# Where the operands of TensorE's products lie in a partition: places modulo 256 bytes instead of modulo 128

## The chip, the cores and the metric

One core of one Trainium2 chip runs the whole kernel. The metric is the device time of one execution in microseconds (us), the median of several runs. The profile is of one further execution.

## The reference

A two-layer decoder trunk on x of 256 x 1024 in float32. Every layer is a mixer between two half-step SwiGLU feed-forward blocks, each with an RMSNorm ahead of it; a last RMSNorm ends it. Layer 0 mixes with a chunked spatial gating unit, layer 1 with stick-breaking attention on keys and values that are made from x ahead of layer 1.

```python
D_MODEL = 1024; SEQ = 256; D_FF = 2816; D_A = 2048; SB_HEADS = 16; SB_KV_HEADS = 4
def swiglu(h, w_in, w_out):
    gate, up = jnp.split(h @ w_in, 2, axis=-1)
    return (jax.nn.silu(gate) * up) @ w_out
for i in range(2):
    if i == 1:
        k, v = split(rms_norm(x, kv_norm) @ w_kv)
    x = x + 0.5 * swiglu(rms_norm(x, ffn_norm[i, 0]), ffn_w_in[i, 0], ffn_w_out[i, 0])
    h = rms_norm(x, mix_norm[i])
    if i == 0:
        u, v = split(gelu(h @ a_w_in)); v = spatial(layer_norm(v))   # W_s causal in chunks of 128
        x = x + (u * v) @ a_w_out
    else:
        x = x + stick_breaking_attention(h @ b_w_q, k, v) @ b_w_o
    x = x + 0.5 * swiglu(rms_norm(x, ffn_norm[i, 1]), ffn_w_in[i, 1], ffn_w_out[i, 1])
return rms_norm(x, final_norm)
```

## The kernel before

x stands transposed in SBUF, as xT of 128 partitions x 8 chunks x 256 tokens. Every float32 operand of a product is split into two parts, hi (rounded to the type float32r) and lo (the rest), and `mm3` (lines 156 to 162) makes one product out of three on TensorE: the lo part of the first operand by the hi part of the second (L160), hi by lo (L161) and hi by hi (L162); the first operand is the loaded one. In each of the three one operand is **loaded** into the array (128 columns of 4 bytes, 512 bytes of each partition) and the other is **moved** through it (256 columns, 1024 bytes of each partition, or 512 columns, 2048 bytes). In this text "a product" is one such instruction pair, a weight load (PEld in the profile) and a matmul (PE).

Worked out from the loops, the kernel has 7540 products with 256 moved columns and 294 with 512, besides 157 small float32 ones (transposes, column sums, the spatial mix).

Weights come in 333 units of 128 x 1024 float32 through the class `Weights`: SP issues the DMA into `raw` seven units ahead, ACT makes `whi` (L85) and VectorE `wlo` (L87) up to five units ahead, and TensorE takes unit after unit in a fixed order. The stages in order are the feed-forward blocks a (tags ga, ua, ya), then the v half of the gating unit (v), its u half with mix and output (uu, mix, ys), block b, the key and value projections (kT and v again), block c, attention with the q and o projections (q, z, at, o, yo) and block d (gd, ud, yo).

Which operand is moved differs by stage. In the first half of a feed-forward block (`project`) the activations xnh and xnl are moved and the weights loaded; in its second half (`Residual.add`) hh and hl are moved and the weights loaded. In the v stage, in the value projection (`project_rows`) and in the second half of block d (`out_add`) it is the weights that are moved, and the activations are loaded.

All tiles are laid out one after another in each partition, by pools in the order of the code. So a tile's place in the partition follows from the sizes of those ahead of it, and two small pools (`gap`), the padded size of `eps` and the argument `place` of `Weights.add` shift it. What counts for the change is the place modulo 256 bytes. Before, it is this (a weight buffer has 4224 bytes, 16.5 times 256, so that neighbouring buffers differ by 128):

| tile | place modulo 256, before | after |
|---|---|---|
| xnh, xnl (moved; loaded in the v stage) | 128 | 192 |
| hh, hl, q, a0, a1 (moved; q and block d's h loaded) | 192 | 192 |
| whi, wlo of the in-weights, loaded | 64 or 192 by buffer | 80 |
| whi, wlo of the out-weights, loaded | 0 or 128 by buffer | 80 |
| whi, wlo, moved: v stage and values | 64 or 192 by buffer | 48 |
| whi, wlo, moved: block d, out | 0 or 128 by buffer | 48 |
| xkh, xkl, oT (moved; xk loaded for the values) | 192 | 192 |
| kz (moved) | 128 | 48 |
| vd (loaded) | 128 | 80 |

The place of the moved operand less that of the loaded one, modulo 256, is thus 64 or 192 before in 7722 products, 0 in 56 and 128 in 56. The 0 and 128 are those of the key and value projections and of the small mask product in attention (later by identr).

Of the kernel before, what the change touches and what calls it, by code (L numbers as in the profile page):

```python
# [8 lines left out]
F32 = mybir.dt.float32  # L9
F32R = mybir.dt.float32r  # L10
# [5 lines left out]
P = 128  # L16
T = 256
D = 1024
KC = D // P
DFF = 2816  # L20
NPAIR = DFF // 256
DA = 2048
UNIT = 1024
# [3 lines left out]
RAW_AHEAD = 7  # L27
SPLIT_AHEAD = 5
WARM = 6, 10

# [6 lines left out]
class Weights:  # L39
# [14 lines left out]
        self.loaded = 0  # L54
        self.split = 0

    def add(self, source, place=0):
        self.sources.append(source)
        self.places.append(place)
        return len(self.sources) - 1  # L60
# [5 lines left out]
    def run_to(self, load, split):  # L66
        nc = self.nc
        while self.loaded < min(load, len(self.sources)):
            i = self.loaded
            raw = self.pools[0].tile([P, UNIT], F32, tag="raw", name=f"raw{i}")  # L70
            src = self.sources[i]
            view = raw if len(src.shape) == 2 else raw.rearrange("p (k c) -> p k c", k=src.shape[1])
            nc.sync.dma_start(view, src)
            self.raw[i] = raw
            self.loaded += 1
        while self.split < min(split, len(self.sources)):
            i = self.split
            raw = self.raw.pop(i)
            hi, lo = (
                pool.tile([P, UNIT + 32], F32R, tag=f"w{p}", name=f"w{p}{i}")[:, self.places[i] : self.places[i] + UNIT]  # L80
                for pool, p in zip(self.pools[1:], ("hi", "lo"))
            )
            for c in range(0, UNIT, self.piece):
                cc = slice(c, c + self.piece)
                ins = nc.scalar.copy(hi[:, cc], raw[:, cc])  # L85
                self.order(ins)
                ins = nc.vector.tensor_sub(lo[:, cc], raw[:, cc], hi[:, cc].bitcast(F32))  # L87
                self.order(ins)
                if self.behind:
                    self.keep_order(ins)  # L90
                    self.behind -= 1
            self.parts[i] = hi, lo
            self.split += 1
# [10 lines left out]
def trunk(  # L104
# [22 lines left out]
    out = out[0]  # L127

    def gap(name, size):


        pool = ctx.enter_context(tc.tile_pool(name=name, bufs=1))
        pool.tile([P, size // 4], F32, name=f"{name}t")

    const = ctx.enter_context(tc.tile_pool(name="const", bufs=1))
    act = ctx.enter_context(tc.tile_pool(name="act", bufs=1))
    gap("gapw", 32)
    rawp = ctx.enter_context(tc.tile_pool(name="rawp", bufs=7))
    hip = ctx.enter_context(tc.tile_pool(name="hip", bufs=9))
    lop = ctx.enter_context(tc.tile_pool(name="lop", bufs=9))  # L140
    gap("gaph", 128)
    hp = ctx.enter_context(tc.tile_pool(name="hp", bufs=4))
    scr = ctx.enter_context(tc.tile_pool(name="scr", bufs=8))
    small = ctx.enter_context(tc.tile_pool(name="small", bufs=3))
# [9 lines left out]
    def scratch(name, width=512):  # L154
        return scr.tile([P, width], F32, tag="scr", name=name, padded_shape=[P, 516])

    def mm3(o, a, b, first, last):

        (ah, al), (bh, bl) = a, b
        nc.tensor.matmul(o, al, bh, start=first, stop=False, skip_group_check=True)  # L160
        nc.tensor.matmul(o, ah, bl, start=False, stop=False, skip_group_check=True)  # L161
        nc.tensor.matmul(o, ah, bh, start=False, stop=last, skip_group_check=True)  # L162
# [15 lines left out]
    W = Weights(tc, rawp, hip, lop)  # L178

    def cols(w, c0, kh):  # L180
        return w[kh * 512 : (kh + 1) * 512, c0 : c0 + 256].rearrange("(k p) c -> p k c", p=P)

    def rows(w, r0):
        return w[r0 : r0 + P, :]

    def plan_in_out(n, ins, w_out):


        steps = {}
        for j in range(n + 1):  # L190
            if j < n:
                steps["in", j] = [[W.add(cols(w, c0 + 256 * j, kh)) for w, c0 in ins] for kh in range(2)]
            if j:
                steps["out", j - 1] = [W.add(rows(w_out, 256 * (j - 1) + P * m), 16) for m in range(2)]
        return steps

    def plan_ffn(i, s):
        return plan_in_out(NPAIR, [(ffn_w_in[i, s], 0), (ffn_w_in[i, s], DFF)], ffn_w_out[i, s])

    plan00 = plan_ffn(0, 0)  # L200
    plan_v = [[W.add(cols(a_w_in[0], DA + 256 * j, kh)) for kh in range(2)] for j in range(8)]
    plan_u = {}
    for step in U_STEPS:
        kind, j = step
        if kind == "in":
            plan_u[step] = [W.add(cols(a_w_in[0], 256 * j, kh)) for kh in range(2)]
        elif kind == "out":
            plan_u[step] = [W.add(rows(a_w_out[0], 256 * j + P * m), 16) for m in range(2)]
    plan01 = plan_ffn(0, 1)
    plan_kv = [[W.add(cols(w_kv, 256 * j, kh)) for kh in range(2)] for j in range(2)]  # L210
    plan10 = plan_ffn(1, 0)
    plan_q = [[W.add(cols(b_w_q[0], 256 * j, kh)) for kh in range(2)] for j in range(4)]
    plan_o = [W.add(rows(b_w_o[0], P * b), 16) for b in range(8)]
    plan11 = plan_ffn(1, 1)


    xin = {}
# [17 lines left out]
    for i, group in enumerate(ROWS):  # L235
        r0 = 0
        for name, ap in group:
            n = ap.shape[0]
# [16 lines left out]
    def warm_up(n):  # L255

        bank = gbank("warm")
        for _ in range(n):
            W.order(nc.tensor.matmul(bank[:, :P], ones, ones, start=True, stop=True))


    def transpose_gains(i):
        n = gT[i].shape[1]
        pgain = gbank(f"pgain{i}")
        nc.tensor.transpose(pgain[:, :n], rowsb[i], ident[:n, :n])
        nc.vector.tensor_copy(gT[i], pgain[:, :n])
# [34 lines left out]
            nc.scalar.activation(s, xT[:, d, :], AF.Square)  # L301
            nc.gpsimd.tensor_add(acc, acc, s)  # L302

    eps = const.tile([P, 1], F32, name="eps", padded_shape=[P, 32])
    nc.vector.memset(eps, RMS_EPS)

    def newton(o, root, v, w):
# [36 lines left out]
    def load_x(hf):  # L344

        for d in range(hf * 4, hf * 4 + 4):
            ptr = ybank(f"ptr{d}")
            for tt in range(2):
                W.order(
                    nc.tensor.transpose(  # L350
                        ptr[:, tt * P : (tt + 1) * P], xin[tt, hf][:, (d % 4) * P : (d % 4 + 1) * P], ident
                    )
                )
            if d % 2:
                W.order(nc.vector.tensor_copy(xT[:, d, :], ptr[:, :T]))
            else:
                W.order(nc.scalar.copy(xT[:, d, :], ptr[:, :T]))
        for d in range(hf * 4, hf * 4 + 4):
            prepare(d, [(("ffn", 0), xnh, xnl)], False)
            if d % 2 == 0:  # L360
                s = scratch(f"sqx{d}", T) if d else acc
                nc.gpsimd.tensor_mul(s, xT[:, d, :], xT[:, d, :])
                if d:
                    nc.gpsimd.tensor_add(acc, acc, s)
            if d == 2:
                W.piece = 512
                W.run_to(0, 1)
                W.piece = UNIT
        W.run_to(0, 2)
        for d in range(hf * 4 + 1, hf * 4 + 4, 2):  # L370
            square(d)

    W.strict = True
    warm_up(WARM[0])
    transpose_gains(0)
    load_x(0)
    warm_up(WARM[1])

# [8 lines left out]
    class Residual:  # L387
# [8 lines left out]
        def add(self, w, h, first, last, ds=range(KC)):  # L396
            for d in ds:
                mm3(
                    self.at(d), tuple(t[:, d * P : (d + 1) * P] for t in w), h, first and d % 2 == 0, last
                )  # L400
# [234 lines left out]
    for kind, j in U_STEPS:  # L635
# [4 lines left out]
        else:  # L640
            h = hs.pop(j)
            for m in range(2):
                w = W.get(plan_u["out", j][m], UNIT)
# [8 lines left out]
    att = ExitStack()  # L652
    at = att.enter_context(tc.tile_pool(name="att", bufs=1))
    at.tile([P, 8], F32, name="gapk")
    kz = [at.tile([P, 4, 2, T], F32R, name=f"kz{p}") for p in "hl"]
    vd = [at.tile([P, 2, 4, 2, 64], F32R, name=f"vd{p}") for p in "hl"]
    at.tile([P, 16], F32, name="gapx")
    xkh = at.tile([P, KC, T], F32R, tag="bigh", name="xkh")
    xkl = at.tile([P, KC, T], F32R, tag="bigl", name="xkl")
    for t in kz:  # L660
        nc.gpsimd.memset(t.bitcast(F32), 0.0)

    laterf = at.tile([P, 2, P], F32, name="laterf")
    later = at.tile([P, 2, P], F32R, name="later")
    identr = at.tile([P, P], F32R, name="identr")
    nc.gpsimd.memset(laterf, 0.0)
# [1 line left out]
        laterf, laterf, pattern=[[0, 2], [-1, P]], compare_op=ALU.is_gt, fill=-(2.0**100), base=0, channel_multiplier=1  # L668
# [201 lines left out]
    for tt in range(2):  # L870
# [20 lines left out]
        r = small.tile([P, 2], F32, tag="fr", name=f"fr{tt}")  # L891
# [40 lines left out]
```

## Time and profile before

| | |
|---|---|
| median of 3 runs | 982.39 us (981.85 to 983.96) |
| the profiled execution | 983.58 us |
| its span, first to last instruction | 981.9 us |
| TensorE (PE) busy | 968.1 us, 99% |
| VectorE (DVE) busy | 641.8 us, 65% |
| ScalarE (ACT) busy | 503.4 us, 51% |
| GpSimd (POOL) busy | 70.4 us, 7% |
| HBM traffic | 181 GB/s over the span |

A matmul's own duration in the profile is modelled and reaches over the start of the next, so it says little. What TensorE spends on a product is read from the starts in the timeline, or from the number of instructions in a window.

### The profile page before, as it was taken

How to read it: one execution, taken by the hardware profiler on the slowest of the kernel's cores; microseconds unless marked ns; L12 is line 12 of the kernel's file. 1: busy time of each engine (PE TensorE's matmuls, PEld its weight loads, DVE VectorE, ACT ScalarE, POOL GpSimd, SP SyncE). 2: the span in 40 equal slices, each digit the busy share in tenths (PEclk: the TensorE clock that was granted, in tenths of full speed). 3: DMA queues.
4: the chain of work that ended last, by engine and by line, in shares of the span. 5: the costliest groups of instructions: out<-in, count | busy, mean ns of one | idle time of the engine just before them, and what ended most of it. 6: DMA issues, size and time to landing. Idle time of an engine off the chain costs nothing.

```text
span 981.9 us, 19299 instructions
## 1 busy us (share of the span) xinstructions
PE 968.1 (99%) x8058; PEld 949.4 (97%) x8058; DVE 641.8 (65%) x823; ACT 503.4 (51%) x691; POOL 70.4 (7%) x98
## 2 busy tenths in 40 slices
PE   8999999999999999999999999999999999999996
PEld 8999999999999999999999999999998999999996
DVE  6865675675866775656569756565689775565653
ACT  6643434474644564444448534343488774444433
POOL 4100000020000310000002000000032120000002
PEclk9999999999999999999999999999999999999999
DMA  9967566647555457575654866666644346656511
GB/s 293 331 196 210 173 194 190 191 136 236 176 190 173 151 175 212 175 211 178 211 176 138 258 190 194 190 193 190 201 150 129 101 148 196 208 179 205 182 43 44
DMA packets 135207, 179.55 MB, mean 183 GB/s; under 512 B 5624, under 2 KB 119376, under 8 KB 135120
## 3 DMA queue, kind: packets, MB, share of 16 engines
q1 hardware_dynamic: 134768, 177.76, 58.1%
q8 instruction: 63, 1.03, 0.4%
q0 software_dynamic: 192, 0.52, 0.2%
q14 instruction: 24, 0.20, 0.1%
q10 hardware_dynamic: 160, 0.05, 0.0%
HBM read 176.73 MB, written 1.05 MB: 181 GB/s over the span
## 4 chain that ended last, share of the span: by engine, by line
PE 90%; DVE 5%; ACT 2%; DMA 1%; issue 1%; SPq 0%; POOL 0%; ACTq 0%; DVEq 0%; POOLq 0%
PE yo L160 3%; PE yo L162 3%; PE yo L161 3%; PE gc L162 2%; PE uc L162 2%; PE gc L161 2%; PE gc L160 2%; PE uc L161 2%; PE gb L162 2%; PE gb L161 2%; PE gb L160 2%; PE uc L160 2%; PE ub L162 2%; PE ub L161 2%; PE ub L160 2%; PE ud L162 2%
## 5 line engine op out<-in xcount | busy, mean ns | idle before, releaser
L85 ACT CAST whi<-raw 128x1024 fp32r<-128x1024 f32 (+1 forms) x333 | 342.3, 1044 | 379.6 <-issue 194.5
L87 DVE TENSOR_TENSOR wlo<-raw,whi 128x1024 fp32r<-128x1024 f32 (+1 forms) x333 | 401.6, 1223 | 195.1 <-ACT whi L85 194.2
L302 POOL TENSOR_TENSOR acc<-acc,sq 128x256 f32<-128x256 f32 x39 | 33.9, 869 | 375.5 <-ACT sq L301 373.6
L161 PE MATMUL ga<-xnl,whi 128*128 128x256 f32 x176 | 49.1, 279 | 1.0 <-DVE xnl L289 1.0
L160 PE MATMUL ga<-xnh,wlo 128*128 128x256 f32 x176 | 49.9, 283 | 0.0
L160 PE MATMUL ua<-xnh,wlo 128*128 128x256 f32 x176 | 48.8, 277 | 0.5 <-DVE wlo L87 0.5
L160 PE MATMUL ya<-hha,wlo 128*128 128x256 f32 x176 | 48.9, 278 | 0.2 <-DVE xT L411 0.2
L160 PE MATMUL yc<-hhc,wlo 128*128 128x256 f32 x176 | 48.9, 278 | 0.1
L160 PE MATMUL gb<-xnh,wlo 128*128 128x256 f32 x176 | 49.0, 278 | 0.0
L160 PE MATMUL gd<-xnh,wlo 128*128 128x256 f32 x176 | 48.9, 278 | 0.0
L160 PE MATMUL yb<-hhb,wlo 128*128 128x256 f32 x176 | 48.9, 278 | 0.0
L160 PE MATMUL gc<-xnh,wlo 128*128 128x256 f32 x176 | 48.9, 278 | 0.0
L162 PE MATMUL ga<-xnh,whi 128*128 128x256 f32 x176 | 48.9, 278 | 0.0
L162 PE MATMUL gc<-xnh,whi 128*128 128x256 f32 x176 | 48.8, 277 | 0.0
L162 PE MATMUL uc<-xnh,whi 128*128 128x256 f32 x176 | 48.8, 277 | 0.0
L161 PE MATMUL gc<-xnl,whi 128*128 128x256 f32 x176 | 48.7, 277 | 0.0
L162 PE MATMUL gd<-xnh,whi 128*128 128x256 f32 x176 | 48.7, 277 | 0.0
L162 PE MATMUL gb<-xnh,whi 128*128 128x256 f32 x176 | 48.7, 277 | 0.0
L162 PE MATMUL ud<-xnh,whi 128*128 128x256 f32 x176 | 48.7, 277 | 0.0
L161 PE MATMUL gb<-xnl,whi 128*128 128x256 f32 x176 | 48.7, 277 | 0.0
L161 PE MATMUL uc<-xnl,whi 128*128 128x256 f32 x176 | 48.7, 277 | 0.0
L161 PE MATMUL gd<-xnl,whi 128*128 128x256 f32 x176 | 48.7, 277 | 0.0
(294 smaller groups left out, 3327.2 us busy)
## 6 DMA issues: line engine op xcount, KB each, us to landing
raw<-in_ffn_w_in_dram SPq DMA_DIRECT2D x176, 512.0 KB, 4.6
raw<-in_ffn_w_out_dram SPq DMA_DIRECT2D x88, 512.0 KB, 4.2
raw<-in_a_w_in_dram SPq DMA_DIRECT2D x32, 512.0 KB, 4.4
raw<-in_a_w_out_dram SPq DMA_DIRECT2D x16, 512.0 KB, 3.3
raw<-in_b_w_q_dram SPq DMA_DIRECT2D x8, 512.0 KB, 4.5
raw<-in_b_w_o_dram SPq DMA_DIRECT2D x8, 512.0 KB, 4.2
raw<-in_w_kv_dram SPq DMA_DIRECT2D x4, 512.0 KB, 4.5
xin<-in_x_dram SPq DMA_DIRECT2D x4, 256.0 KB, 4.9
```

The lines of the kernel that those rows point to most:

```text
L85: ins = nc.scalar.copy(hi[:, cc], raw[:, cc])
L87: ins = nc.vector.tensor_sub(lo[:, cc], raw[:, cc], hi[:, cc].bitcast(F32))
L160: nc.tensor.matmul(o, al, bh, start=first, stop=False, skip_group_check=True)
L161: nc.tensor.matmul(o, ah, bl, start=False, stop=False, skip_group_check=True)
L162: nc.tensor.matmul(o, ah, bh, start=False, stop=last, skip_group_check=True)
L302: nc.gpsimd.tensor_add(acc, acc, s)
```

## The change

Every weight buffer becomes 4352 bytes, 17 times 256, so that all weight buffers have the same place modulo 256, and a unit is put 208 bytes into its buffer if it will be loaded (LOADED) or 176 bytes if it will be moved (MOVED). The padding of eps and the pool gaph move the activations to 192. The tiles kz and vd for the keys and values become one tile each, with 176 and 208 bytes ahead of their content. In all 7818 products but the 16 of the mask, the moved operand's place less the loaded one's is then 112 modulo 256. Since kz, vd and the buffers need more room, the tile laterf (the mask before rounding) is no longer a tile of its own: it takes one of the eight scratch buffers.

```diff
+LOADED, MOVED = 52, 44
...
-    def add(self, source, place=0):
+    def add(self, source, place=LOADED):
...
-                pool.tile([P, UNIT + 32], F32R, tag=f"w{p}", name=f"w{p}{i}")[:, self.places[i] : self.places[i] + UNIT]
+                pool.tile([P, UNIT + 64], F32R, tag=f"w{p}", name=f"w{p}{i}")[:, self.places[i] : self.places[i] + UNIT]
...
-    gap("gaph", 128)
+    gap("gaph", 64)
...
-                steps["out", j - 1] = [W.add(rows(w_out, 256 * (j - 1) + P * m), 16) for m in range(2)]
+                steps["out", j - 1] = [W.add(rows(w_out, 256 * (j - 1) + P * m), place) for m in range(2)]
...
-    plan_v = [[W.add(cols(a_w_in[0], DA + 256 * j, kh)) for kh in range(2)] for j in range(8)]
+    plan_v = [[W.add(cols(a_w_in[0], DA + 256 * j, kh), MOVED) for kh in range(2)] for j in range(8)]
...
-            plan_u[step] = [W.add(rows(a_w_out[0], 256 * j + P * m), 16) for m in range(2)]
+            plan_u[step] = [W.add(rows(a_w_out[0], 256 * j + P * m)) for m in range(2)]
...
+        [W.add(cols(w_kv, 256 * j, kh), place) for kh in range(2)] for j, place in enumerate((LOADED, MOVED))
...
-    plan_o = [W.add(rows(b_w_o[0], P * b), 16) for b in range(8)]
-    plan11 = plan_ffn(1, 1)
+    plan_o = [W.add(rows(b_w_o[0], P * b)) for b in range(8)]
+    plan11 = plan_ffn(1, 1, MOVED)
...
-    eps = const.tile([P, 1], F32, name="eps", padded_shape=[P, 32])
+    eps = const.tile([P, 1], F32, name="eps", padded_shape=[P, 48])
...
-    kz = [at.tile([P, 4, 2, T], F32R, name=f"kz{p}") for p in "hl"]
-    vd = [at.tile([P, 2, 4, 2, 64], F32R, name=f"vd{p}") for p in "hl"]
+    kzs = at.tile([P, 2 * 8 * T + 64], F32R, name="kz")[:, 44 : 44 + 2 * 8 * T]
+    vds = at.tile([P, 2 * 16 * 64 + 64], F32R, name="vd")[:, 52 : 52 + 2 * 16 * 64]
...
-    laterf = at.tile([P, 2, P], F32, name="laterf")
+    laterf = scratch("laterf", T).rearrange("p (n s) -> p n s", n=2)
```

On TensorE, VectorE, ScalarE and SP the instructions stand in the same order as before, with the same shapes. Only POOL's order moves, in one place: at the end of the gating unit, where POOL prepares the attention's mask (laterf, later) and adds up the squares of the new x (acc) for block b's norm. Before, with what each waits for:

```order
L661 MEMSET kzh 128x2048 [waits DVE_49,DMAHW4_49,PE_49,Activation_49]
L661 MEMSET kzl 128x2048
L666 MEMSET laterf 128x256
L671 CAST identr<-ident 128x128
L667 AFFINE_SELECT laterf<-laterf 128x256 [waits Pool_49]
L670 CAST later<-laterf 128x256 [waits Pool_49]
L302 TENSOR_TENSOR acc<-acc,sq_4100 128x256 [waits Activation_49]
L302 TENSOR_TENSOR acc<-acc,sq_4112 128x256 [waits Activation_49,Pool_49]
```

And now the same place in the changed kernel, from the fifth of the seven sums on:

```order
L307 TENSOR_TENSOR acc<-acc,sq_4148 128x256 [waits Activation_49,Pool_49]
L307 TENSOR_TENSOR acc<-acc,sq_4160 128x256 [waits Activation_49,Pool_49]
L674 MEMSET laterf 128x256 [waits DVE_49]
L675 AFFINE_SELECT laterf<-laterf 128x256 [waits Pool_49]
L307 TENSOR_TENSOR acc<-acc,sq_4172 128x256 [waits Activation_49]
L678 CAST later<-laterf 128x256 [waits Pool_49]
```

The two instructions that fill laterf have moved from ahead of the seven sums to between the sixth and the last, and the first of them now waits for VectorE, which used that scratch buffer before. The cast to later follows the last sum.

## Rows read from the trace of the kernel before

**Rows 1.** The page: busy times, slices of the clock, costliest groups.
```profile
PE 968.1 (99%) x8058; PEld 949.4 (97%) x8058; DVE 641.8 (65%) x823; ACT 503.4 (51%) x691; POOL 70.4 (7%) x98
...
PE 90%; DVE 5%; ACT 2%; DMA 1%; issue 1%; SPq 0%; POOL 0%; ACTq 0%; DVEq 0%; POOLq 0%
```

**Rows 2.** Waits of TensorE alone: total us, times, longest.
```profile
PE o L160 <- DVE a0l L166: 1.6, 2, 0.9
PE warm L259 <- DVE eps L305: 1.1, 1, 1.1
PE ga L161 <- DVE xnl L289: 1.0, 1, 1.0
```

**Rows 3.** Busy time by stage: a, v, u, b, keys and values, c, attention, d.
```profile
30.00:198.00 168.00, 168.00 (x1464) 166.68 (x1463) 110.69 (x135) 77.93 (x93) 1.65 (x2) 1.00 0.66 206
199.00:256.00 57.00, 57.00 (x487) 56.95 (x487) 40.11 (x61) 36.39 (x51) 4.19 (x5) 1.00 0.59 180
256.00:339.00 83.00, 83.00 (x719) 82.55 (x718) 57.16 (x70) 37.07 (x44) 5.70 (x6) 1.00 0.56 182
340.00:525.00 185.00, 185.00 (x1622) 184.74 (x1621) 117.03 (x144) 91.21 (x120) 8.37 (x11) 1.00 0.62 188
525.90:533.00 7.10, 6.84 (x57) 6.50 (x56) 5.97 (x15) 7.07 (x12) 2.42 (x3) 1.00 0.23 74
536.00:716.00 180.00, 180.00 (x1575) 179.81 (x1574) 113.14 (x129) 83.46 (x102) 4.75 (x10) 1.00 0.66 204
717.00:790.00 73.00, 70.99 (x555) 67.77 (x554) 61.84 (x91) 58.11 (x114) 18.44 (x31) 1.00 0.39 123
```

**Rows 4.** Timeline of TensorE in block b: start, duration, line, tiles.
```profile
440.08 0.28 PE L162 MATMUL gb<-xnh,whi 128*128 128x256 f32 x1
440.19 0.28 PE L160 MATMUL ub<-xnh,wlo 128*128 128x256 f32 x1
...
441.44 0.28 PE L162 MATMUL gb<-xnh,whi 128*128 128x256 f32 x1
```

**Rows 5.** Timeline of the weight loads, same place.
```profile
440.08 0.19 PEld L160 LDWEIGHTS ub<-xnh,wlo 128*128 128x128 f32 x1
440.20 0.19 PEld L161 LDWEIGHTS ub<-xnl,whi 128*128 128x128 f32 x1
```

**Rows 6.** Timeline of TensorE in the v stage, first and last of 19.
```profile
211.78 0.28 PE L162 MATMUL v<-whi,xnh 128*128 128x256 f32 x1
...
213.90 0.28 PE L162 MATMUL v<-whi,xnh 128*128 128x256 f32 x1
```

**Rows 7.** Timeline of TensorE in the key projection, first and last of 18.
```profile
526.01 0.29 PE L160 MATMUL kT<-xkh,wlo 128*128 128x256 f32 x1
...
528.04 0.27 PE L162 MATMUL kT<-xkh,whi 128*128 128x256 f32 x1
```

**Rows 8.** The 16 transposes ahead of block d's output: timeline, merged; durations in ns.
```profile
813.32 1.91 PE L839 MATMUL xb<-ident,xT 128*128 128x128 f32 x16
...
L839 PE MATMUL xb<-ident,xT x16: 272/273/273, 813.3 to 815.0; 128*128 128x128 f32 x16
```

**Rows 9.** Timeline of TensorE: products with 512 columns, first and last of 7.
```profile
850.04 0.40 PE L160 MATMUL yo<-whi,hld 128*128 128x512 f32 x1
...
851.43 0.39 PE L160 MATMUL yo<-whi,hld 128*128 128x512 f32 x1
```

**Rows 10.** Timeline of TensorE around the column sums of block b's norm.
```profile
346.69 0.28 PE L160 MATMUL ub<-xnh,wlo 128*128 128x256 f32 x1
346.80 0.28 PE L161 MATMUL ub<-xnl,whi 128*128 128x256 f32 x1
346.91 0.28 PE L162 MATMUL ub<-xnh,whi 128*128 128x256 f32 x1
347.03 0.50 PE L325 MATMUL pstf<-ones,acc 128*128 128x1 f32 x4
347.59 0.28 PE L161 MATMUL gb<-xnl,whi 128*128 128x256 f32 x1
...
348.54 0.28 PE L160 MATMUL ub<-xnh,wlo 128*128 128x256 f32 x1
```

**Rows 11.** Timeline of POOL, same place.
```profile
336.29 0.30 POOL L666 MEMSET laterf<- 128x256 f32 x1
...
336.79 0.40 POOL L667 TENSOR_SCALAR_AFFINE_SELECT laterf<-laterf 128x256 f32<-128x256 f32 x1
...
342.43 4.35 POOL L302 TENSOR_TENSOR acc<-acc,sq 128x256 f32<-128x256 f32 x5 [0.73 <-ACT sq L301]
```

More of the change, by code (lines that the diff above doesn't have):

```diff
@@ L184, in rows, with plan_in_out @@
         return w[r0 : r0 + P, :]
-    def plan_in_out(n, ins, w_out):
+    def plan_in_out(n, ins, w_out, place):
         steps = {}
@@ L193, in plan_in_out, with plan_ffn @@
             if j:
-                steps["out", j - 1] = [W.add(rows(w_out, 256 * (j - 1) + P * m), 16) for m in range(2)]
+                steps["out", j - 1] = [W.add(rows(w_out, 256 * (j - 1) + P * m), place) for m in range(2)]
         return steps
-    def plan_ffn(i, s):
-        return plan_in_out(NPAIR, [(ffn_w_in[i, s], 0), (ffn_w_in[i, s], DFF)], ffn_w_out[i, s])
+    def plan_ffn(i, s, place=LOADED):
+        return plan_in_out(NPAIR, [(ffn_w_in[i, s], 0), (ffn_w_in[i, s], DFF)], ffn_w_out[i, s], place)
     plan00 = plan_ffn(0, 0)
-    plan_v = [[W.add(cols(a_w_in[0], DA + 256 * j, kh)) for kh in range(2)] for j in range(8)]
+    plan_v = [[W.add(cols(a_w_in[0], DA + 256 * j, kh), MOVED) for kh in range(2)] for j in range(8)]
     plan_u = {}
@@ L207, in trunk @@
         elif kind == "out":
-            plan_u[step] = [W.add(rows(a_w_out[0], 256 * j + P * m), 16) for m in range(2)]
+            plan_u[step] = [W.add(rows(a_w_out[0], 256 * j + P * m)) for m in range(2)]
     plan01 = plan_ffn(0, 1)
-    plan_kv = [[W.add(cols(w_kv, 256 * j, kh)) for kh in range(2)] for j in range(2)]
+    plan_kv = [
+        [W.add(cols(w_kv, 256 * j, kh), place) for kh in range(2)] for j, place in enumerate((LOADED, MOVED))
+    ]
     plan10 = plan_ffn(1, 0)
     plan_q = [[W.add(cols(b_w_q[0], 256 * j, kh)) for kh in range(2)] for j in range(4)]
-    plan_o = [W.add(rows(b_w_o[0], P * b), 16) for b in range(8)]
-    plan11 = plan_ffn(1, 1)
+    plan_o = [W.add(rows(b_w_o[0], P * b)) for b in range(8)]
+    plan11 = plan_ffn(1, 1, MOVED)
     xin = {}
@@ L654, in trunk @@
     at.tile([P, 8], F32, name="gapk")
-    kz = [at.tile([P, 4, 2, T], F32R, name=f"kz{p}") for p in "hl"]
-    vd = [at.tile([P, 2, 4, 2, 64], F32R, name=f"vd{p}") for p in "hl"]
+    kzs = at.tile([P, 2 * 8 * T + 64], F32R, name="kz")[:, 44 : 44 + 2 * 8 * T]
+    kzs = kzs.rearrange("p (w k r t) -> p w k r t", w=2, k=4, r=2)
+    vds = at.tile([P, 2 * 16 * 64 + 64], F32R, name="vd")[:, 52 : 52 + 2 * 16 * 64]
+    vds = vds.rearrange("p (w n k r e) -> p w n k r e", w=2, n=2, k=4, r=2)
+    kz, vd = ([t[:, w] for w in range(2)] for t in (kzs, vds))
     at.tile([P, 16], F32, name="gapx")
```

## The prediction

> **What bounds the kernel now.** I read the busy line and the chain on the page first: TensorE is busy for 968.1 of 981.9 us, and 90% of the chain that ended last is TensorE's [rows 1]. Next the waits of TensorE alone: the longest three groups are 1.6, 1.1 and 1.0 us [rows 2]. So other engines hardly hold it up, and the time is the number of products by the time between two of them. That spacing is the thing to read, and the busy time hides it, since one matmul's modelled duration reaches over the next two starts.
>
> In block b the thirteen rows from 440.08 to 441.44 us give 1.36 us for 12 steps, 113.3 ns each [rows 4], and each weight load starts at or within 10 ns after a matmul and lasts until past the next start [rows 5]: the load for the next product and the moving of the present one read SBUF together, all the time. The stage table gives the same by count. Dividing the stretch by the instructions: block a 168.00/1464 = 114.8 ns, block b 185.00/1622 = 114.1, block c 180.00/1575 = 114.3, the v stage 57.00/487 = 117.0 [rows 3]. In these four stretches DVE is busy for at most 71% and ACT for at most 64%, the DMA engines for 0.59 to 0.66, and the granted clock is 1.00 in every stage [rows 3]: the spacing isn't the clock's doing (2.4 GHz is granted), nor a missing operand's.
>
> **What spacing could be.** 256 columns at 2.4 GHz are 106.7 ns. Three kinds of rows bound what else is there.
> - Lowest: the 16 transposes ahead of block d's output. They move 128 float32 columns, half the bytes of a product, each with a load beside it, and 1.91 us less one modelled duration of 0.273 over 15 steps is 109.1 ns [rows 8]. Nothing in the trace runs a pair faster.
> - 113.3 ns: the products whose two operands are 64 bytes apart modulo 128 [rows 4].
> - Highest: the key projection, where the difference is 0 in some products and 128 in the others: 2.03 us for 17 steps, 119.4 ns [rows 7].
>
> So place matters: the key projection has the same shapes, engines and order as block b, and takes 6.1 ns more. But place as before isn't all of it. In the v stage, with differences of 64 and 192 only, 18 steps take 2.12 us, 117.8 ns [rows 6]; there the moved operand's own place changes between 64 and 192 as buffers alternate. And in block b the spacing is 113 ns right up to four small column sums, and from 347.59 to 348.54 us, eight steps later, 118.8 ns with the places unchanged [rows 10]. The fast spacing is a state in which the two streams fall into step; an interruption loses it for a while, and it is not found at all where the places are wrong. 512 columns show more of it: six steps in 1.39 us are 231.7 ns, against 213.3 for the columns alone [rows 9], though a load of 128 columns can share only a part of them.
>
> **What the change does to the products.** It gives all but 16 products one difference, 112, which the trace of before doesn't have. The rows allow two readings. If the effect repeats every 256 bytes, 112 is near the far side of the circle: from 0 (119.4) to 64 (113.3) the gain is 0.095 ns a byte, and the same line at 112 would give 108.8, under the 109 that nothing beats. If it repeats every 128 bytes, 112 is 16 from 0, and the line gives 119.4 - 16 x 0.095 = 117.9. Ends: 109 and 117.9. For the first reading stands the v stage, where moved places 128 apart do disturb; for the second, that the products with 128 in the key projection are no faster than those with 0. I take the first, because the second also needs the 56 products with 128 to be slow by their own place and not because of those with 0 between them, and the rows behind the interruption in block b show that a product can be slow for what came before it [rows 10]. I put the value at 110.0, not at the 109 floor, since the moved stream has twice the bytes of the transposes'.
>
> The sum, then:
> - 7540 products of 256 columns from 113.3 to 110.0: 7540 x 3.3 = 24.9 us.
> - Strays above 113.3, counting the waits among them, are what the stretches hold beyond count x 113.3: 2.1 us in block a, 1.8 in v, 1.5 in u, 1.2 in b, 1.6 in c [rows 3], 8.2 in all. They come back after each interruption; with one place everywhere I let half go: 4.1 us.
> - 294 products of 512 columns from 231.7 to 2 x 110.0: 3.4 us.
> - Lost again: attention, where 70.99 of 73.00 us are busy and chains through ACT and DVE pace the steps [rows 3], gives back half of its own 463 x 3.3 = 1.5 us, so 0.8.
> - POOL's order: filling laterf (0.30 + 0.40 us) now stands ahead of the last of the sums, of which the final five run back to back until 346.78; the column sums start on TensorE at 347.03 [rows 10, 11]. The cover is 0.25 us, so up to 0.45 us are added there, and behind the column sums on TensorE stands the rest of block b's first projection. Once the products are faster, the cover is gone and it is 0.7. Lower bound 0, since POOL no longer does these two instructions ahead of the sums; I take 0.5.
> - Everything else costs nothing. The split into hi and lo writes at other places, but ACT and DVE have at least 29% of each of blocks a, b, c and of the v and u stages free [rows 3], and would have a fifth free if the two were 10% slower. Merging kz and vd changes no instruction, and SP's queue stands in the same order.
>
> 24.9 + 4.1 + 3.4 - 0.8 - 0.5 = 31.1 us. The profiled execution took 983.58 us around its span of 981.9, 1.2 above the median of the runs; I take the gain off the median: 982.4 - 31.1 = 951.3 us.
>
> The Trainium skill has a price for the floor: TensorE: Matmul & The Clock Gate, under Back-to-back issue gap, gives N/2.4 + 2.5 ns for a warm matmul by itself, 109.2 for 256 columns. By it, as an estimate, the first term would be 7540 x 4.1 = 30.9 us instead of 24.9. [...]
>
> **The rivals.**
> - *In step everywhere, but no faster in step.* 113.3 is what such a product costs with a float32r operand of 4 bytes a column, and the new places only bring the v stage, the projections and the restarts to it. For it: 113.3 is the same whether the loaded place alternates or not. Gain: 8.2 us of strays, and for 512 columns 294 x (231.7 - 226.6) = 1.5; some 973 us. Against it: 512 columns cost more than twice 113.3, so what slows the stream isn't a fixed fee per product.
> - *The place doesn't matter.* What I read as place is phase alone, set by interruptions, as around the column sums [rows 10]; then nothing moves but POOL's half microsecond: 982 to 983 us. Against it: in 18 rows of the key projection and 19 of the v stage the fast spacing is never found. The same page of the Trainium skill, in Part 2 on loading, says outright that loading the next weights takes no read bandwidth from the running matmul, since TensorE has two read ports; by that rule this is the case that comes. The 119.4 against 113.3 speaks against it.
> - *Slower: the period is 128.* The new difference is 16 bytes from the bad one, the products run at 117.9 throughout, and blocks a to c never find the fast state: 7540 x 4.6 = 34.7 us more, less the 8.2 of strays that are already in it: about 1009 us. It decides once the common spacing is above 114.4 (the mean of the large stages now).
>
> **How the numbers follow.** Forecast 44%, in step but no faster 22%, no effect 14%, slower 20%. The forecast's own range goes from the 109 floor with all strays gone and 512 columns at 218 (982.4 - 7540 x 4.3/1000 - 8.2 - 4.0 = 938) to 112 ns (967). For 8 in 10 the range must take in the second and third case and leaves out the slower one: 936 to 992 us. A measurement of this kernel tells 0.2%, 2 us, from no change. Faster by more than that: the first two cases, 66%. Within it: 13%. Slower: 21%, with POOL's new order and a spacing just over 114.4 in it.
>
> **What would show it.** Right: twelve steps in block b's steady stretch take 1.32 us instead of 1.36; the v stage and the key projection run like block b; a 20 us stretch of block b holds some 182 products instead of 176; the products behind the column sums are as fast as those ahead; 512 columns come to about 220 ns. TensorE's busy share stays at 99%. The second case shows 113.3 in all stages; the third the same mixture as before; the slower one 117 to 119 in blocks a to c. What would make the prediction wrong beside these is a new wait: if the spacing falls and TensorE then stands behind wlo in several places, ACT and DVE have become the bound, which 144 and 120 instructions with 117.03 and 91.21 us in 185.00 [rows 3] don't suggest.

## The result: 1014.7 us against 982.6 us, slower

The changed kernel takes 1014.66 us (median of 5 runs, 1011.74 to 1015.8), the kernel before 982.6 us in the same comparison (981.85 to 983.96): a ratio of 1.032, interval 1.031 to 1.033. The forecast was 951.3 us, with a range of 936 to 992.

The page of the changed kernel, as in [rows 1]: TensorE (PE) is still busy for 99%, and the chain that ended last is still TensorE's.

```profile
PE 998.0 (99%) x8058; PEld 979.8 (97%) x8058; DVE 641.9 (64%) x823; ACT 503.0 (50%) x691; POOL 67.8 (7%) x98
...
PE 93%; DVE 3%; ACT 2%; DMA 1%; issue 1%; SPq 0%; POOL 0%; ACTq 0%; DVEq 0%; POOLq 0%
```

DVE and ACT have the same busy times as before; the 28 us by which the profiled executions differ are TensorE's alone. The stages of the changed kernel, in the columns of [rows 3]: blocks a, the v stage, u, block b, keys and values, block c, attention. The stages begin later by now, so the windows do too.

```profile
30.00:198.00 168.00, 168.00 (x1392) 166.85 (x1391) 103.14 (x122) 73.07 (x84) 0.00 (x0) 1.00 0.63 196
207.00:264.00 57.00, 57.00 (x496) 56.95 (x495) 40.66 (x62) 37.04 (x52) 3.89 (x4) 1.00 0.60 189
264.30:347.30 83.00, 83.00 (x697) 82.59 (x696) 54.92 (x67) 35.70 (x43) 3.80 (x3) 1.00 0.54 174
349.00:534.00 185.00, 185.00 (x1563) 184.92 (x1561) 110.59 (x128) 84.77 (x103) 6.51 (x10) 1.00 0.59 183
542.20:549.30 7.10, 6.84 (x58) 6.52 (x57) 5.97 (x15) 7.07 (x12) 2.38 (x3) 1.00 0.22 74
552.20:732.20 180.00, 180.00 (x1522) 179.97 (x1521) 107.99 (x119) 80.06 (x94) 3.32 (x8) 1.00 0.63 197
741.00:814.00 73.00, 71.52 (x551) 68.47 (x550) 61.31 (x90) 57.12 (x111) 16.70 (x30) 1.00 0.40 123
```

Divide each stretch by its matmuls, as the prediction did: block a 168.00/1392 = 120.7 ns (114.8 before), u 119.1 (115.4), b 118.4 (114.1), c 118.3 (114.3). The v stage goes the other way: 57.00/496 = 114.9 against 117.0. The clock is at 1.00 everywhere, and DMA's share is within 0.03 of what it was [rows 3].

The timeline of TensorE in the changed kernel, as in [rows 4, 6, 7, 9, 10]: first and last rows of a steady stretch in the v stage, around block b's column sums, in block b, in the key projection, in the value projection right behind it, and of 512 columns.

```profile
219.93 0.28 PE L163 MATMUL v<-whi,xnl 128*128 128x256 f32 x1
...
221.97 0.28 PE L163 MATMUL v<-whi,xnl 128*128 128x256 f32 x1
...
356.34 0.28 PE L165 MATMUL ub<-xnh,whi 128*128 128x256 f32 x1
356.46 0.50 PE L330 MATMUL pstf<-ones,acc 128*128 128x1 f32 x4
...
450.00 0.28 PE L163 MATMUL gb<-xnh,wlo 128*128 128x256 f32 x1
...
451.42 0.28 PE L163 MATMUL gb<-xnh,wlo 128*128 128x256 f32 x1
...
542.30 0.28 PE L163 MATMUL kT<-xkh,wlo 128*128 128x256 f32 x1
...
544.32 0.28 PE L165 MATMUL kT<-xkh,whi 128*128 128x256 f32 x1
...
547.71 0.28 PE L163 MATMUL v<-whi,xkl 128*128 128x256 f32 x1
...
549.41 0.28 PE L163 MATMUL v<-whi,xkl 128*128 128x256 f32 x1
...
856.02 0.39 PE L163 MATMUL yo<-whi,hld 128*128 128x512 f32 x1
...
857.41 0.39 PE L163 MATMUL yo<-whi,hld 128*128 128x512 f32 x1
```

Twelve steps of block b take 1.42 us, 118.3 ns; the key projection is at 2.02/17 = 118.8. But 18 steps of the v stage take 2.04 us, 113.3 ns, and the value projection, a few us behind the key projection, is at 1.70/15 = 113.3. All four have the same difference, 112. They differ in where the pair lies: blocks and keys have the moved operand at 192 and the loaded one at 80, v and values have 48 and 192. So a difference of 112 is neither good nor bad by itself.

The intervals from each TensorE start to the next, added up by the tile that is written, give the whole in us (the last column is an experiment's, below):

| stage | before | changed | 208 against 16 |
|---|---|---|---|
| block a | 184.5 | 192.3 | 183.3 |
| v stage and values | 51.9 | 50.3 | 50.4 |
| u, mix and output | 96.3 | 99.5 | 95.7 |
| block b | 181.2 | 188.1 | 180.9 |
| block c | 181.4 | 188.0 | 180.2 |
| block d, first half | 120.9 | 125.7 | 120.5 |
| block d, 512 columns | 56.9 | 56.9 | 57.2 |

### The profile page after: what moved, and what is told of

It is laid out like the page before. It is cut to its first block, busy times and chain, and to the rows that moved or that the text cites. A ratio compares the mean times of both kernels' runs of the same rounds, so it can differ in the third digit from the quotient of the medians.

```text
span 1010.0 us, 19299 instructions
## 1 busy us (share of the span) xinstructions
PE 998.0 (99%) x8058; PEld 979.8 (97%) x8058; DVE 641.9 (64%) x823; ACT 503.0 (50%) x691; POOL 67.8 (7%) x98
## 4 chain that ended last, share of the span: by engine, by line
PE 93%; DVE 3%; ACT 2%; DMA 1%; issue 1%; SPq 0%; POOL 0%; ACTq 0%; DVEq 0%; POOLq 0%
PE yo L163 3%; PE yo L165 3%; PE yo L164 3%; PE gd L163 2%; PE gb L163 2%; PE ud L163 2%; PE gd L164 2%; PE gd L165 2%; PE ub L163 2%; PE ud L165 2%; PE gb L165 2%; PE uc L165 2%; PE uc L164 2%; PE ub L164 2%; PE ud L164 2%; PE gc L163 2%
## 5 line engine op out<-in xcount | busy, mean ns | idle before, releaser
L165 PE MATMUL ua<-xnh,whi 128*128 128x256 f32 x176 | 50.0, 284 | 0.0
L164 PE MATMUL ua<-xnl,whi 128*128 128x256 f32 x176 | 50.0, 284 | 0.0
L164 PE MATMUL ya<-hla,whi 128*128 128x256 f32 x176 | 50.0, 284 | 0.0
L163 PE MATMUL ud<-xnh,wlo 128*128 128x256 f32 x176 | 49.7, 282 | 0.0
L165 PE MATMUL ya<-hha,whi 128*128 128x256 f32 x176 | 49.7, 284 | 0.0
L164 PE MATMUL ub<-xnl,whi 128*128 128x256 f32 x176 | 49.6, 282 | 0.0
```

## The experiments

In what follows a pair (m, l) is the place of the moved and of the loaded operand modulo 256. "Steady" is the mean of the last steps of a group (15, where nothing else is said), after the run-in, which is the first products, until the spacing repeats. The granted clock of the small kernels is 1.00 over their whole span, and that of the large ones is 1.00 in every stretch shown.

**1. A map of all places in steps of 16.** The trunk is left out; 256 groups of 32 products each, one for each pair.

```python
for b in range(16):            # loaded place 16 b
    for a in range(16):        # moved place 16 a
        o = bank(f"m{L[a]}l{L[b]}")
        for i in range(32):
            mm(o, 256, a, b, i, 31)
```

> This kernel leaves out the whole trunk (its output is x): it runs 256 groups of 32 products of 256 columns, one group for each place modulo 256 in steps of 16 of the moved operand (16) by the loaded one (16), on TensorE alone. By difference (theory D, period 128): the spacing depends on moved less loaded alone, slow (117 to 120 ns) at 0, 16, 112, 128, 144 and 240, fast (113.3) at 64 and 192, so the map has diagonals. By the loaded operand's own place (theory A): rows, slow where the loaded place is no multiple of 32 or 64, whatever the moved one is. By the sum (theory S, the load is read from its end): the map has diagonals the other way, fast at a sum of 240 and of 64 and 192, slow at 16. If a group shows 109 to 111 anywhere, the floor can be lowered by place alone.

The steady spacing, middle value over the eight loaded places of a kind, in ns:

| moved less loaded | 0 | 16 | 32 | 48 | 64 | 80 | 96 | 112 | 128 | 144 | 160 | 176 | 192 | 208 | 224 | 240 |
|---|---|---|---|---|---|---|---|---|---|---|---|---|---|---|---|---|
| loaded at a multiple of 32 | 120.0 | 118.7 | 116.7 | 118.4 | 113.3 | 119.7 | 119.7 | 113.3 | 118.7 | 118.7 | 117.3 | 119.2 | 113.3 | 119.1 | 118.5 | 117.1 |
| loaded 16 past one | 118.2 | 120.1 | 118.1 | 116.7 | 118.3 | 118.2 | 120.0 | 120.1 | 120.0 | 120.0 | 116.5 | 118.7 | 113.3 | 122.9 | 119.7 | 118.4 |

30 of the 256 pairs are at 113.3, none is under it. The timeline of the map's kernel, merged by group (start, us, products); the letters give the places, a for 0, b for 16, and so on to p for 240, the moved one first:

```profile
328.80 3.81 PE L37 MATMUL mblf<-moved,loaded 128*128 128x256 f32 x32
...
370.55 4.00 PE L37 MATMUL mmlf<-moved,loaded 128*128 128x256 f32 x32
...
749.09 3.93 PE L37 MATMUL malm<-moved,loaded 128*128 128x256 f32 x32
...
760.51 3.82 PE L37 MATMUL mdlm<-moved,loaded 128*128 128x256 f32 x32
...
779.33 3.80 PE L37 MATMUL milm<-moved,loaded 128*128 128x256 f32 x32
```

Take one modelled duration of 0.28 off and divide by 31 steps: (192, 80), the pair of the changed kernel's blocks, 120.0; (16, 80) with a difference of 192, 113.9; (48, 192), the pair of its v stage, 114.2 with its run-in. So the map has both halves of the result in it. None of the three theories orders it: with a period of 128, 112 and 240 would be alike (113.3 and 117.1, loaded at a multiple of 32), as would 64 and 192 (118.3 and 113.3, loaded 16 past one); and neither the loaded place alone nor the sum of both sorts the fast pairs. In these steps the map is ordered by the difference modulo 256 and by whether the loaded place is a multiple of 32. One difference is mixed: of the eight pairs with 64 and a loaded multiple of 32, six are at 113.3 and two at 117.8, among them (0, 192), malm above.

**2. Patterns of hi and lo.** The trunk is left out. Groups in mm3's order of three, hi and lo at places 128 apart as neighbouring buffers have them before the change; 512 columns; and six pairs repeated six times behind column sums.

```python
def three(name, n, mh, ml, lh, ll, count):
    o = bank(name)
    for i in range(0, count, 3):
        mm(o, n, mh, ll, i, count - 1)
        mm(o, n, ml, lh, i + 1, count - 1)
        mm(o, n, mh, lh, i + 2, count - 1)
```

> This kernel leaves out the trunk too: it runs triples in the order of the real kernel (moved hi by loaded lo, lo by hi, hi by hi). 16 groups with the loaded lo part 128 behind its hi part and moved at 128, 16 with the moved lo part 128 behind its hi part and loaded at 128, 16 with 512 columns, loaded at 192, and six repeats each, behind a short interruption, of the places that block b has before (moved 128, loaded 64 and 192) and after (192, 80), the v stage before (moved 64 and 192, loaded 128) and after (48, 192), and (192, 64) and (192, 128). If place alone decides, the six repeats agree with each other, block b before gives 113.3 and after 119 to 120, the v stage before 117 to 118 and after 113.3. If it is the phase after an interruption, the six repeats of one pair differ among themselves.

With the moved operand at 128 and the loaded hi and lo 128 apart, one of 16 places is steady at 113.3 (hi at 192, lo at 64), the others at 117.8 to 121.1; with the moved hi and lo 128 apart, as the v stage had them before [rows 6], none of 16: 116.7 to 120.0 (both over the last 24 steps). All six repeats of a pair agree within 0.4 ns. That is what place alone would give; but all six stand behind the same column sums, so it doesn't test the entry. Two of them, behind the same column sums (hi and lo at 64 and 192 under a moved 128; then (48, 192)):

```profile
293.39 5.95 PE L37 MATMUL raa<-moved,loaded 128*128 128x256 f32 x48
...
305.74 5.74 PE L37 MATMUL rac<-moved,loaded 128*128 128x256 f32 x48
```

The mean of 47 steps is 120.6 and 116.2, with a first step of 0.20 us and, in the second, a run-in of ten to twelve products. Block b before the change has both arrangements of the loaded parts in turn, as buffers go round (hi at 192 and lo at 64, hi at 64 and lo at 192): tried alone the one is at 113.3 and the other at 118.7 to 119.1, where 113.3 was expected; in the trunk the steady stretch is at 113.3 throughout [rows 4]. This is left open here.

**3 and 4. The changed kernel with loaded weights at other places.** Only the constant is changed, so only the loaded weights move; the v stage and the values stay at (48, 192).

```diff
-LOADED, MOVED = 52, 44
+LOADED, MOVED = 64, 44     # third run: loaded at 128, difference 64
+LOADED, MOVED = 48, 44     # fourth run: loaded at 64, difference 128
```

> The changed kernel with loaded weights at 128 instead of 80 (LOADED 64): difference 64, sum 64, loaded place a multiple of 64. All three theories expect 113 to 114 ns in blocks a to c and some 972 to 984 us, since everything else of the change, POOL's order and the larger buffers, is then priced at under 1 us. If it stays near 1014 us, the cause is not the place of the loaded weights.

> The changed kernel with loaded weights at 64 instead of 80 (LOADED 48): difference 128, sum 0, loaded place a multiple of 64. Theory D (period 128): slow as at 0, 119 ns, some 1012 to 1020 us. Theory A: fast, 972 to 980 us. Theory S has the sum 0 between 240, which is fast, and 16, which is slow: anything between.

Loaded at 128 the kernel takes 1005.88 us (ratio 1.0229, interval 1.0212 to 1.0246), at 64 it takes 1012.81 us (1.0303, 1.0287 to 1.0318). Block b in the third run, then in the fourth, in the columns of [rows 3]:

```profile
349.00:534.00 185.00, 185.00 (x1568) 184.66 (x1567) 110.92 (x130) 85.29 (x105) 5.02 (x9) 1.00 0.61 186
```

```profile
349.00:534.00 185.00, 185.00 (x1558) 184.79 (x1557) 109.63 (x126) 84.21 (x102) 5.41 (x9) 1.00 0.60 182
```

In the 185 us the one runs 1568 matmuls, 118.0 ns, the other 1558, 118.7; the v stage, which was not moved, holds 498 and 497 in its 57 us, 114.5 and 114.7, close to the changed kernel's 114.9. 118.7 is the map's figure for 128. For 64 the map has 113.3, and 972 to 984 us were expected from all three theories; the trunk doesn't come to it: in blocks a to d the products stand at 117.8. So the loaded place moves the time, by 9 us here, but this run does not yet show that place is all of it.

**5. Ways of entering.** The trunk is left out. Ten pairs, each entered in 14 ways: behind one product of 16 to 240 columns, behind column sums, or behind a wait for ScalarE.

```python
PAIRS = [(12, 8), (12, 0), (12, 5), (3, 12), (13, 6), (8, 4), (8, 12), (13, 1), (9, 13), (12, 4)]
for k, (a, b) in enumerate(PAIRS):     # places 16 a and 16 b
    for kick in range(14):
        run(f"q{L[k]}{L[kick]}", a, b, kick)
```

> This kernel leaves out the trunk: ten pairs of places, each entered in 14 ways (one product of 16 to 240 columns ahead, four small column sums, or a wait for ScalarE), 36 products each. If place alone decides, the 14 entries of a pair end at the same spacing: 113.3 for (192, 128), (192, 0), (48, 192), (208, 96), (128, 64), (128, 192), (208, 16), (144, 208) and 118 to 119 for (192, 80) and (192, 64). If a pair has two steady states and the entry picks one (which would explain 117.5 in the changed kernel with loaded weights at 128, against 113.3 for the same places alone), some pairs show 113.3 from some entries and 117 to 118 from others. I expect that of (192, 128) and (128, 64), and that (48, 192), which is steady in the v stage, ends at 113.3 from all.

| pair | difference | steady, over 14 entries |
|---|---|---|
| (192, 128), (128, 64) | 64 | 117.8 from all |
| (192, 0) | 192 | 113.3 from 6, 117.8 from 8 |
| (128, 192) | 192 | 113.3 from 4, 117.8 from 10 |
| (48, 192), (208, 96) | 112, loaded at a multiple of 32 | 113.3 from all |
| (208, 16), (144, 208) | 192, loaded 16 past one | 113.3 from all, soonest (run-in of 1 to 10 products; 3 to 14 for the row above) |
| (192, 80) | 112, loaded 16 past one | 118.3 or 120.0 |
| (192, 64) | 128 | 118.8 to 120.0 |

The timeline, merged by group: (192, 0) entered behind products of 96 and of 112 columns (qb), (192, 80) behind one of 80 (qc), (48, 192) behind one of 80 (qd).

```profile
106.76 4.51 PE L37 MATMUL qbf<-moved,loaded 128*128 128x96 f32 x37
111.11 4.38 PE L37 MATMUL qbg<-moved,loaded 128*128 128x112 f32 x37
...
163.50 4.54 PE L37 MATMUL qce<-moved,loaded 128*128 128x80 f32 x37
...
225.13 4.39 PE L37 MATMUL qde<-moved,loaded 128*128 128x80 f32 x37
```

The two first rows have the same places and stay 0.13 us apart over 36 products: there are two steady levels for these pairs, and what came before picks one. That bears out the prediction's idea of a state that hangs on what came before [rows 10], with the correction that pairs differ in whether they have a choice at all. Nor do 14 entries show every choice: (192, 128), at 117.8 from all of them and in the third run, was at 113.3 in the map and in all six repeats of the second experiment.

**6. The choice in the trunk: loaded weights at 0.** Again only the constant (LOADED = 32), for (192, 0).

> The changed kernel with loaded weights at 0 (LOADED 32): difference 192, loaded place a multiple of 32. By the map alone 113.3 in blocks a to c, 972 to 980 us. If entries decide and 192 is as open to the slow state as 64 was, 117 to 118 and some 1005 us.

993.17 us (ratio 1.0128, interval 1.009 to 1.0166), with executions near 990 and others near 997. Stretches of blocks b and c, in the columns of [rows 3]:

```profile
350.00:500.00 150.00, 150.00 (x1323) 149.95 (x1323) 92.97 (x98) 68.78 (x78) 0.00 (x0) 1.00 0.64 203
550.00:700.00 150.00, 150.00 (x1276) 150.00 (x1276) 86.32 (x92) 64.24 (x72) 0.00 (x0) 1.00 0.60 189
```

150 us hold 1323 matmuls in block b and 1276 in block c, 113.4 and 117.6 ns: one execution, equal places and equal code, and each block stays for all of its stretch on the level that it got.

**7 and 8. All places 16 bytes further, and the pair that has no choice.** Activations and hidden rows go to 208. For this the tiles for hi and lo become one tile, with 16 bytes ahead of the content; weights that are moved go to 144, for (144, 208). The key projection and attention's output projection, 240 products, have their moved operands at 192 still and their loaded weights at 0. The loaded weights are at 96 in the seventh run, which is the changed kernel's own difference of 112, and at 16 in the eighth, difference 192.

```diff
-LOADED, MOVED = 52, 44
+LOADED, MOVED = 56, 4      # eighth run: 36, 4
+SHIFT = 4
...
-    xnh = act.tile([P, KC, T], F32R, name="xnh")
-    xnl = act.tile([P, KC, T], F32R, name="xnl")
+    xn = act.tile([P, 2 * KC * T + 64], F32R, name="xn")[:, SHIFT : SHIFT + 2 * KC * T]
+    xnh, xnl = (xn[:, w * KC * T : (w + 1) * KC * T].rearrange("p (k t) -> p k t", t=T) for w in range(2))
...
+    def hpair(name):
+        t = hp.tile([P, 2 * 512 + 64], F32R, tag="h", name=name)[:, SHIFT : SHIFT + 1024]
+        return t[:, :512], t[:, 512:]
```

> The whole computation, with the activations, the hidden rows and the loaded weights of the changed kernel all put 16 bytes further: activations at 208, loaded weights at 96, so that the difference stays 112 and the loaded operand lies at a multiple of 32. (The moved weights go to 144, which against activations at 208 is a difference of 192; the 288 products of the attention's key and output projections go to 192 against 0.) Theory 1, the map's rule (difference mod 256, and whether the loaded place is a multiple of 32): the products of blocks a to d, of u and of q, which stood at 118 to 120, come out at 113.3 after a run-in of some ten products at each entry, 114 to 115 in the mean; some 6,700 products by 4.5 ns take 30 us off 1014.7, so 980 to 986 us. Theory 2, the difference alone counts and 112 is a slow one in the trunk: still 118 to 120 in the blocks, 1008 to 1016 us. Theory 3, how a stage is entered decides between two steady levels: some stages at 113.3 and others at 117.8, 985 to 1005 us, with a spread over executions as where the loaded weights lay at 0.

> The whole computation, with activations and hidden rows at 208 and loaded weights at 16 (difference 192, the loaded operand 16 past a multiple of 32); moved weights at 144 against activations at 208 (also 192, also 16 past a multiple of 32). In the small kernels such pairs came to 113.3 from all 14 ways of entering, soonest of all pairs. Theory 1, the map's rule: every stage at 113.3 to 114 in the mean, no stage at 117.8; 974 to 980 us, faster than both kernels. Theory 3, the two levels are open to every pair and the entries decide: a mixture of 113.3 and 117.8, 985 to 1000 us. If the place of the operands did not set the time of the trunk (something else in the changed kernel does): 1008 to 1016 us.

(208, 96): 979.33 us, ratio to the kernel before 0.9965, interval 0.9953 to 0.9978. (208, 16): 978.04 us, 0.9954, 0.9939 to 0.9968. Both beat the kernel before, by 3.2 and 4.5 us; the seventh keeps the changed kernel's difference in the blocks and only puts their operands 16 bytes further, and it is 35 us faster. The v stage and block b of the seventh, then block b of the eighth, columns as above:

```profile
199.00:256.00 57.00, 57.00 (x503) 56.95 (x503) 40.74 (x61) 36.65 (x51) 2.73 (x3) 1.00 0.64 195
...
340.00:505.00 165.00, 164.74 (x1451) 164.49 (x1450) 99.97 (x112) 77.38 (x88) 3.86 (x7) 1.00 0.62 192
```

```profile
340.00:505.00 165.00, 164.72 (x1451) 164.47 (x1450) 100.02 (x112) 77.29 (x88) 3.81 (x7) 1.00 0.62 192
```

164.74/1451 = 113.5 ns in block b, strays included, against 114.1 before the change [rows 3] and 118.4 in the changed kernel. The gain over the kernel before is no larger because its blocks were at 113.3 already: for the eighth run the table of stages gives 1.5 in the v stage and the values, 1.2 each in a and c, 0.6 in u, and under half a us elsewhere.

**9. Steps of 4 bytes.** The trunk is left out: the map again, around (208, 16), (192, 0) and (208, 96), and 512 columns under a loaded 208.

```python
for b0 in (0, 96):
    for k in range(9):
        for j in range(9):
            o = bank(f"f{'n' if b0 else 'o'}{L[j]}{L[k]}")
            for i in range(32):
                at(o, 256, 192 + 4 * j, b0 + 4 * k, i, 31)
```

> The trunk is left out; 162 groups of 32 products of 256 columns with moved places 192 to 224 and loaded places 0 to 32, and again with loaded places 96 to 128, both in steps of 4 bytes; then 16 groups of 24 products of 512 columns, loaded at 208, moved at each multiple of 16. Theory C (cells of 16 bytes): what counts is in which 16 bytes a place lies; the products are at 113.3 for moved 208 to 220 with loaded 96 to 108 (difference 112 in cells, loaded in the lower half of a 32), for 208 to 220 with loaded 16 to 28, and for 192 to 204 with loaded 0 to 12, at 116 to 120 elsewhere, with sharp edges at multiples of 16. Theory E (exact places): a shift of both by 4 bytes already loses 113.3, so that only single places in the grid are fast. Theory G (the difference counts to the byte, not the cell): fast along the diagonals with a difference of 112 and 192, whatever the places on them. For 512 columns: the least that the earlier map gave was 226.6 with loaded 192 (moved 176 and 192); against loaded 208 I expect the least at moved 192 or 208, some 227, and 232 at 144, the place in the kernel that beat both.

Neither cells of 16 bytes nor the bare difference: single places. The timeline by group, moved 208 and 212 against loaded 96, then against 100:

```profile
349.14 3.83 PE L40 MATMUL fnea<-moved,loaded 128*128 128x256 f32 x32
352.81 4.08 PE L40 MATMUL fnfa<-moved,loaded 128*128 128x256 f32 x32
...
383.55 3.94 PE L40 MATMUL fneb<-moved,loaded 128*128 128x256 f32 x32
387.32 4.07 PE L40 MATMUL fnfb<-moved,loaded 128*128 128x256 f32 x32
```

(208, 96) is steady at 113.3; four bytes more on the loaded side make 117.7, on the moved side 122.5, on both 122.3. In all 162 pairs of this run 113.3 comes up eight times, each time with the moved operand at a multiple of 16, and the loaded one also at places such as 12, 24, 108 and 116. So "a multiple of 32" orders the places in steps of 16 only and is no law of its own. With 512 columns, 226.7 came up at moved places 16, 64, 112, 176 and 192, and 228.9 at 144.

**10. The 512 columns of block d put at such a place.** In the eighth run's kernel the weights that block d moves go from 144 to 192.

```diff
+WIDE = 16
...
-    plan11 = plan_ffn(1, 1, MOVED)
+    plan11 = plan_ffn(1, 1, WIDE)
```

> The kernel with activations at 208 and loaded weights at 16, and in it only block d's output weights, which are moved with 512 columns (246 products) and with 256 (36 products), put at 192 in place of 144. The fine map gave 226.7 ns for 512 columns at 192 against 208 and 228.9 at 144; the trunk had 232.3 at 144. Theory: the map's place holds in the trunk too, 226.7 to 228 in the mean, so 246 products by 4.3 to 5.6 ns less 36 by some 5: 0.9 to 1.2 us, 976.8 to 977.1 against 978.0. Rival: with 512 columns the level is set by how the stretch is entered and by hi and lo buffers in turn, so the mean stays at 231 to 233 and the time at 978.0 to 978.3.

977.66 us (977.3 to 978.24), against 977.62 to 978.12 in the eighth run: no difference. The 246 products take 57.4 us by the intervals between starts, 233.4 ns each, where they took 57.2 and 232.6. So about the rival's spacing came: the level that the place reaches by itself is not reached in the trunk. What holds it up there was not tried.

## Why the prediction was wrong, step by step

**What bounds the kernel** was read rightly: the time is the number of products by their spacing, place sets the spacing, and the other engines hide behind it in the changed kernel and in the variants.

**The failed step is the choice between two readings**, "I put the value at 110.0", for a difference that the trace of before doesn't have. I laid a line through two points, 119.4 at 0 and 113.3 at 64, and carried it to 112. The map shows that the spacing doesn't fall along a line: for loaded places at multiples of 32 it goes 120.0, 118.7, 116.7, 118.4, 113.3, 119.7, 119.7, 113.3. No pair goes below 113.3, so 24.9 us of the sum could not come at all. The 109.1 that the prediction took for the floor was read from transposes of 128 float32 columns [rows 8], another shape and type, and no product of 256 columns came near it in any run. And in steps of 16, 112 reaches 113.3 only with the loaded operand at a multiple of 32: the prediction reckoned with the difference alone and gave the loaded place no part. The change put it at 80 in blocks a to d, u, keys and q. At 118 to 120 these stages took 7.8 us more in block a, 6.9 in b, 6.6 in c, 4.8 in d's first half and 3.2 in u, by the table of stages.

**Of the rivals**, the slower one had about the time (1009 us, 117.9 ns), but by luck, since its reason falls: with a period of 128 the v stage at the same difference would be slow as well, and it is at 113.3. "In step everywhere, but no faster in step" had the right floor and, in the seventh and eighth runs, its mechanism; its 973 us took all 8.2 us of strays for recoverable and 1.5 more for the 512 columns, and the eighth run has 4.5 in all (982.53 less 978.04), with nothing from the 512 columns (57.2 us against 56.9). "The place doesn't matter" falls: the eighth run has the instructions of the changed kernel in number, shape and order, POOL's too, and its weight buffers of 4352 bytes, only at other places, and takes 36.6 us less. The Trainium skill, TensorE: Matmul & The Clock Gate, in Part 2 on loading, with its two read ports, would have both kernels alike, as the prediction read it; the runs disagree by these 36.6 us, though they don't show where the two streams meet.

**The smaller terms.** Strays: of the 4.1 us only the v stage's part came, 51.9 to 50.3 us. That agrees with the reason given, moved places that no longer alternate (none of the sixteen such patterns tried alone came to 113.3), and (48, 192) is a pair that comes to 113.3 from all entries. The 512 columns were put from 231.7 to 220 and stayed: 1.39 us for six steps, before and after. Attention moved by 0.3 us (q, z, at and o; 0.7 with its output projection); by the loops it has 448 products of 256 columns and not 463, which leaves that term at 0.7. POOL's order cost nothing here. POOL in the changed kernel, around the last sum:

```profile
354.79 0.31 POOL L674 MEMSET laterf<- 128x256 f32 x1
355.18 0.41 POOL L675 TENSOR_SCALAR_AFFINE_SELECT laterf<-laterf 128x256 f32<-128x256 f32 x1
355.55 0.74 POOL L307 TENSOR_TENSOR acc<-acc,sq 128x256 f32<-128x256 f32 x1
```

The last sum ends at 356.29, and TensorE comes to the column sums at 356.46, 0.12 after the product ahead of them: no wait. By the prediction's own reasoning the slower products left POOL the time. In the eighth run block b's products are at 113.3, as before the change, and there the wait is seen. TensorE in it, around the same column sums:

```profile
343.20 0.28 PE L171 MATMUL ub<-xn,whi 128*128 128x256 f32 x1
343.75 0.61 PE L336 MATMUL pstf<-ones,acc 128*128 128x1 f32 x4 [0.28 <-POOL acc L313]
```

0.55 us lie between the starts instead of 0.12, so POOL's order costs 0.43 us there: close to the 0.45 that the prediction worked out for products at the old spacing, and to the 0.5 of its sum.

**What stays open**: why these single places and no others; what makes the kernel before, whose differences of 64 and 192 have two levels, get the lower one in all four blocks, though one of the two arrangements in it, tried alone, ends at 118.7; and why 512 columns don't come to 226.7 in the trunk. The experiments show that the entry picks the level for such pairs, not which entry picks which. In the small kernels the moved operand goes on by 1024 bytes from product to product and the loaded one by 512; whether such steps, and not the places modulo 256 alone, make them differ from the trunk was not tried.

## What to carry to other kernels

Where TensorE runs products back to back, the time between two starts, read from the timeline, says more than the busy share: 113 and 120 ns both read as 99%. For these products, each with a load of its own, the places of the two operands in the partition set it, and no line through known places tells an unknown one: a small kernel that runs all pairs of places shows them, and should also enter each pair in several ways, because a pair that reaches the lower level in one setting may miss it in another. Choose a pair that gets there from every entry ((208, 16) here) and then look stage by stage whether the trunk does too.

## What the runs showed of the hardware

- For products of 128 loaded and 256 moved float32r columns, at a granted clock of 1.00 (2.4 GHz), no run has a steady spacing under 113.3 ns; by place they cost up to 123.5 ns (experiment 9), 9% more.
- Four bytes decide: (208, 96) 113.3, (208, 100) 117.7, (212, 96) 122.5.
- Some pairs have two steady levels, 113.3 and 117.8, and kept the one that they got for 150 us (experiment 6); others come to 113.3 from all 14 entries tried.
- In steps of 16 the steady spacing goes by the difference of the places modulo 256 and by whether the loaded one is a multiple of 32 (experiment 1), with two levels for some pairs; 128 is no period of it.
